# Gate and up products of two FFN half-steps as Strassen blocks, with the down product in three partial passes

## The chip, the cores and the metric

The kernel runs on one core of one Trainium2 chip. The metric is the device time of one execution in microseconds (us); a kernel is judged by the median of its runs. Five engines work side by side and meet at semaphores: PE (TensorE, the matrix products; its weight loads are listed apart as PEld), DVE (VectorE), ACT (ScalarE), POOL (GpSimd) and SP (SyncE), which here only issues DMAs. Each engine works through its own instructions in a fixed order.

## The reference

One layer of a sequence model on x of 512 tokens by 1024 features, in float32:

```python
def swiglu(h, w_gate, w_up, w_down):
    return (jax.nn.silu(h @ w_gate) * (h @ w_up)) @ w_down

x = x + 0.5 * swiglu(rms_norm(x, ffn1_norm), ffn1_w_gate, ffn1_w_up, ffn1_w_down)
x = x + hybrid_mixer(x, ...)
x = x + 0.5 * swiglu(rms_norm(x, ffn2_norm), ffn2_w_gate, ffn2_w_up, ffn2_w_down)
return rms_norm(x, final_norm)
```

`w_gate` and `w_up` are 1024 x 2816, `w_down` is 2816 x 1024. The mixer projects the normed x to 3600 columns, runs a state-space scan on 16 heads and banded attention on 8, and projects back with `w_out`. The change leaves the mixer's arithmetic as it is.

## The kernel before

Activations lie feature-major: 128 features on the partitions, 512 tokens along them, so the model width is 8 tiles (KD) and the FFN width 22 tiles (NF). Every float32 operand of a product is split into two float32r parts, hi and lo, and every product is three matmuls, hi·hi, hi·lo and lo·hi (`mm3`, L130 to L133).

Weights come through `Stream` (L101 to L126): `prepare` has SP load a piece into one of three `raw` buffers, and `wsplit` (L94 to L99) makes the parts, the hi part by a cast on ACT (L96), the lo part by a subtraction on DVE (L98), 128x512 at a time. `get` keeps three pieces ahead of the one in use.

`ffn` (L217 to L256) is one SwiGLU half-step. For each of 22 feature tiles it runs the gate product (`proj` into a PSUM tile of tag `mm`) and the up product (into `aux`): 8 contraction tiles x 3 matmuls of 512 columns each, 48 for both. DVE then multiplies each by the norm's factor (L234, L238), ACT takes the silu (L236), DVE multiplies the two (L240), and ACT and DVE split the result into parts (L242, L243). The norm is not applied to x ahead of the product: `split_act` (L136 to L139) scales x by the norm's weight as it splits it, and the factor 1/sqrt(mean) of a token comes from `rstd_begin` and `rstd_end` (sums of squares on ACT and DVE, L143 to L147, then small DVE steps L154 to L162, diagonals L187, and two matmuls L194 that spread them). Behind all 22 tiles the down product runs 8 output features, each 22 contraction tiles x 3 matmuls in one PSUM accumulation, and one DVE instruction adds it to x (L255).

The first tile of FFN 1 stands apart (L289 to L305), interleaved with the arrival of x. Ahead of FFN 2 the second part of the output projection (L808 to L822) adds to x (L820) and splits x for FFN 2. In the last feature of FFN 2 (`last2`) the halves of the tokens go one after the other, by 132 matmuls of 256 columns, so that the final norm of one half lies beside the product of the other.

The order on each engine is that of the program, moved by a scheduler that knows the data and buffers. POOL makes constants at the start, the decay products of the scan (L432) and the bias tiles of attention (L706); in the two FFNs it has nothing.

Of the kernel before, what the change touches and what calls it, by code (L numbers as in the profile page):

```python
# [8 lines left out]
F32 = mybir.dt.float32  # L9
# [21 lines left out]
# columns of the packed per-partition parameter array  # L31
# [6 lines left out]
def hybrid_block(ctx: ExitStack, tc, xT, par, wgu1, wd1, win, wdt, wv, wo, rbt, wgu2, wd2, out):  # L38
# [30 lines left out]
    # the tensor engine's clock rises after some time of work: constants, until the first data is there  # L69
# [6 lines left out]
    # triLE[s, l] = 1 where s <= l ; gt[s', s] = 1 where s' > s  # L76
# [5 lines left out]
    gtf = sb("fa", [P, P], bufs=2)  # L82
# [3 lines left out]
    # onl[:, 0]: first 64 columns one, onl[:, 1]: last 64 columns one  # L86
# [14 lines left out]
    class Stream:  # L101
        """Weights in the order in which they are used: loaded in pieces of up to 4 KB a partition,
        split exactly into two float32r parts in halves of those, some halves ahead of their use."""

        def __init__(self, look=3):
            self.src, self.done, self.used, self.look, self.raw = [], [], 0, look, None

        def add(self, dram, n, c):
            """dram: [128, n, c]"""
            sub = SEQ // c  # L110
            for a in range(0, n, sub):
                self.src.append((dram if a == 0 else None, n, c, a, min(n, a + sub)))

        def prepare(self):
            dram, n, c, a, b = self.src[len(self.done)]
            if dram is not None:
                self.raw = sb("raw", [P, n, c], bufs=3)
                nc.sync.dma_start(out=self.raw, in_=dram)
            self.done.append(wsplit(self.raw[:, a:b]))
# [29 lines left out]
    def rsqrt_tiny(v, n):  # L149
        """v^-1/2 on [128, n]"""  # L150
# [20 lines left out]
    def rstd_begin(acc, n):  # L171
        """1/sqrt(mean + eps) per token: on the diagonals of [128, tile, 128], and as columns"""
# [6 lines left out]
    def diag_parts(r, n, dh, dl):  # L179
        """columns r as diagonals, in two exact parts"""  # L180
# [22 lines left out]

    def xw_tiles():
        return ([sb(f"xwh{k}", [P, SEQ], F32R) for k in range(KD)],
                [sb(f"xwl{k}", [P, SEQ], F32R) for k in range(KD)])

# [1 line left out]
    def ffn_weights(wgu, wd, f0=0, o1=KD):  # L209
        for ft in range(f0, NF):  # L210
            ws.add(wgu[ft, 0], KD, P)
            ws.add(wgu[ft, 1], KD, P)
        for o in range(o1):
            for a, b in ((0, 8), (8, 16), (16, 22)):
                ws.add(wd[o, :, a:b, :], b - a, P)

    def ffn(xh, xl, norm, hslots, after, first=None, last=None):  # L217
        hh, hl = [], []
        for ft in range(NF):
            if ft == 0:  # L220
                pss = first or [proj(xh, xl, mmps()), proj(xh, xl, aux())]
                # the norm's factor comes between the next tile's products
                dg = None if first else norm()
                nxt = [proj(xh, xl, mmps())]
                dg = dg or norm()
                if first:
                    nxt.append(proj(xh, xl, aux()))
                rs = rstd_end(dg)
            elif ft == 1:
                pss = nxt if first else nxt + [proj(xh, xl, aux())]  # L230
            else:
                pss = [proj(xh, xl, mmps()), proj(xh, xl, aux())]
            a = sb("fa", [P, SEQ], bufs=2)
            V.tensor_tensor(out=a, in0=pss[0], in1=rs, op=ALU.mult)  # L234
            s = sb("fs", [P, SEQ], bufs=2)
            S.activation(out=s, in_=a, func=AF.Silu)  # L236
            u = sb("fu", [P, SEQ], bufs=2)
            V.tensor_tensor(out=u, in0=pss[1], in1=rs, op=ALU.mult)  # L238
            h = sb("fh", [P, SEQ], bufs=2)
            V.tensor_tensor(out=h, in0=s, in1=u, op=ALU.mult)  # L240
            hi, lo = hslots[ft]()
            S.copy(out=hi, in_=h)  # L242
            V.tensor_tensor(out=lo, in0=h, in1=f(hi), op=ALU.subtract)  # L243
            hh.append(hi)
            hl.append(lo)
        for o in range(KD):
            if o == KD - 1 and last:
                last(hh, hl)
                break
            ps = mmps()  # L250
            for a in range(0, NF, 4):
                wh, wl = ws.get()
                for k in range(a, min(a + 4, NF)):
                    mm3(ps, wh[:, k - a], wl[:, k - a], hh[k], hl[k], k == 0, k == NF - 1)
            V.scalar_tensor_tensor(out=x[:, o], in0=ps, scalar=0.5, in1=x[:, o], op0=ALU.mult, op1=ALU.add)  # L255
            after(o)  # L256

    def proj(xh, xl, ps):
        for k in range(KD):
            if k % 4 == 0:  # L260
                wh, wl = ws.get()
            mm3(ps, wh[:, k % 4], wl[:, k % 4], xh[k], xl[k], k == 0, k == KD - 1)
        return ps

    # slots that are also used side by side as one tile
# [66 lines left out]
    ffn(x1h, x1l, norm1, [pair_slot(2 * i, 2 * i + 1) for i in range(NF)], after1, first=first)  # L332
    xh, xl = x2
# [1 line left out]
    # order of the feature tiles of the projection (win is laid out in the same order)  # L335
# [17 lines left out]
    def proj_gen(ah, al, done):  # L353
        """one feature tile, in pieces of two contraction tiles"""
# [11 lines left out]
    def conv(ci, dst, ps):  # L366
        u = sb("fa", [P, SEQ], bufs=2)
# [15 lines left out]
    def bc(g):  # L383
        """B and C of a group, of which the first is evacuated after most of the second's products"""
# [8 lines left out]
    def bc_products(g):  # L393
        # token-major B of the first three chunks
# [6 lines left out]
        # C.B products with s <= l: cbm[g][s, c, l]  # L401
# [34 lines left out]
    def ssd_in(st):  # L436
# [3 lines left out]
        # token-major x * dt  # L440
# [7 lines left out]
        # D skip, in place of the feature-major x  # L448
# [504 lines left out]
```

## Time and profile before

| | us |
|---|---|
| median of 3 runs (lowest, highest) | 1075.79 (1075.69, 1076.99) |
| span of the profiled execution | 1074.0 |
| FFN 1, first tile | 0 to 18 |
| FFN 1, rest | 18 to 368 |
| projections, scan, attention | 368 to 681 |
| second part of the output projection | 681 to 700 |
| FFN 2 and final norm | 700 to 1074 |

The runs lie some 1.8 us above the span of the profiled execution, which counts from its first instruction to its last. How to read the tables: "busy" is the time in which an engine had an instruction in work; the matmuls overlap in their pipeline, so that one lasts 0.39 us and yet a new one starts each 0.23 us, and the step from start to start is the rate. The clock column is the TensorE clock that was granted, 1.00 for the upper of its two levels, 2.4 GHz.

### The profile page before, as it was taken

To read this page: it belongs to the slowest core of one execution; us is meant where nothing else is said; L and a number is where in the kernel's file an instruction comes from. 1 tells how busy PE (TensorE), PEld (TensorE's weight loads), DVE (VectorE), ACT (ScalarE), POOL (GpSimd) and SP (SyncE) were. 2 spreads that over 40 slices of the span, in tenths; PEclk is the share of its full clock that TensorE was granted. 3 is DMA by queue.
4 is the path that set the end of the run, shared out by engine and by line. 5 is a ranking of instruction groups with operands and counts; after the bars stand their busy time and mean duration, and the time that the engine had idled before them with its cause. 6 is when DMAs were issued, how large, how long until landed. Compare 5 with 4: busy or idle time off the path is not lost.

```text
span 1074.0 us, 13004 instructions
## 1 busy us (share of the span) xinstructions
PE 1059.9 (99%) x4922; PEld 868.4 (81%) x4922; DVE 609.5 (57%) x1131; ACT 463.9 (43%) x805; POOL 56.5 (5%) x61
## 2 busy tenths in 40 slices
PE   9999999999999999999999999999999999999996
PEld 7888888888888787878887777888888888888886
DVE  6644445453334398978858888864444445433333
ACT  6433333333323356646747855543333333333331
POOL 0000000000000003332110111000000000000000
PEclk9999999999999999999999999999999999999998
DMA  6223333223233221212221222223322222333322
GB/s 223 96 98 98 98 99 99 98 93 93 89 98 99 98 79 59 79 60 79 80 98 61 77 81 81 92 81 99 99 98 98 98 99 98 94 89 101 100 69 79
DMA packets 31518, 99.54 MB, mean 93 GB/s; under 512 B 3296, under 2 KB 5600, under 8 KB 31456
## 3 DMA queue, kind: packets, MB, share of 16 engines
q1 hardware_dynamic: 29216, 95.69, 28.0%
q10 hardware_dynamic: 2240, 3.02, 0.9%
q8 instruction: 38, 0.62, 0.2%
q14 instruction: 24, 0.20, 0.1%
HBM read 96.61 MB, written 2.10 MB: 92 GB/s over the span
## 4 chain that ended last, share of the span: by engine, by line
PE 92%; DVE 6%; ACT 1%; issue 0%; DMA 0%; DVEq 0%; ACTq 0%
PE mm L131 21%; PE mm L132 21%; PE mm L133 20%; PE aux L131 8%; PE aux L132 8%; PE aux L133 8%; DVE fs L377 2%; PE aux L759 1%; PE aux L737 1%; DVE wlo L98 1%; PE aux L719 1%; PE aux L501 0%; PE aux L718 0%; PE aux L461 0%; DVE fa L368 0%
## 5 line engine op out<-in xcount | busy, mean ns | idle before, releaser
L96 ACT CAST whi<-raw 128x512 fp32r<-128x512 f32 x354 | 216.3, 612 | 426.1 <-PE mm L132 256.3
L98 DVE TENSOR_TENSOR wlo<-raw,whi 128x512 fp32r<-128x512 f32 x354 | 244.6, 692 | 219.4 <-ACT whi L96 217.9
L131 PE MATMUL mm<-xwh,whi 128*128 128x512 f32 x520 | 209.1, 402 | 1.5 <-ACT whi L96 1.5
L132 PE MATMUL mm<-xwl,whi 128*128 128x512 f32 x520 | 203.5, 391 | 0.0
L133 PE MATMUL mm<-xwh,wlo 128*128 128x512 f32 x520 | 203.0, 390 | 0.0
L131 PE MATMUL mm<-s,whi 128*128 128x512 f32 x482 | 187.7, 390 | 0.0
L132 PE MATMUL mm<-s,whi 128*128 128x512 f32 x482 | 187.7, 389 | 0.0
L133 PE MATMUL mm<-s,wlo 128*128 128x512 f32 x482 | 187.6, 389 | 0.0
L131 PEld LDWEIGHTS mm<-xwh,whi 128*128 128x128 f32 x520 | 98.0, 188 | 23.7 <-issue 2.8
L133 PEld LDWEIGHTS mm<-xwh,wlo 128*128 128x128 f32 x520 | 97.6, 188 | 20.8
L132 PEld LDWEIGHTS mm<-xwl,whi 128*128 128x128 f32 x520 | 97.8, 188 | 20.2 <-issue 1.2
L133 PEld LDWEIGHTS mm<-s,wlo 128*128 128x128 f32 x482 | 90.5, 188 | 19.1
L131 PEld LDWEIGHTS mm<-s,whi 128*128 128x128 f32 x482 | 90.5, 188 | 19.0 <-ACT s L763 0.2
L132 PEld LDWEIGHTS mm<-s,whi 128*128 128x128 f32 x482 | 90.4, 188 | 18.8 <-DVE s L764 0.2
L131 PE MATMUL aux<-xwh,whi 128*128 128x512 f32 x176 | 68.7, 390 | 0.0
L133 PE MATMUL aux<-xwh,wlo 128*128 128x512 f32 x176 | 68.6, 390 | 0.0
L132 PE MATMUL aux<-xwl,whi 128*128 128x512 f32 x176 | 68.5, 389 | 0.0
L131 PE MATMUL aux<-s,whi 128*128 128x512 f32 x176 | 68.5, 389 | 0.0
L133 PE MATMUL aux<-s,wlo 128*128 128x512 f32 x176 | 68.5, 389 | 0.0
L132 PE MATMUL aux<-s,whi 128*128 128x512 f32 x176 | 68.5, 389 | 0.0
L238 DVE TENSOR_TENSOR fu<-aux,rstd 128x512 f32<-128x512 f32 x44 | 30.4, 691 | 62.5 <-PE aux L133 62.5
L234 DVE TENSOR_TENSOR fa<-mm,rstd 128x512 f32<-128x512 f32 x44 | 30.4, 691 | 60.5 <-PE mm L133 60.5
(234 smaller groups left out, 1203.1 us busy)
## 6 DMA issues: line engine op xcount, KB each, us to landing
raw<-wgu SPq DMA_DIRECT2D x86, 512.0 KB, 3.3
raw<-wd SPq DMA_DIRECT2D x32, 512.0 KB, 3.5
raw<-win SPq DMA_DIRECT2D x28, 512.0 KB, 3.3
raw<-wd SPq DMA_DIRECT2D x16, 384.0 KB, 3.1
raw<-wo SPq DMA_DIRECT2D x12, 512.0 KB, 3.6
x<-xT SPq DMA_DIRECT2D x8, 256.0 KB, 5.1
raw<-wv SPq DMA_DIRECT2D x4, 512.0 KB, 3.9
fu<-rbt ACTq DMA_DIRECT2D x8, 256.0 KB, 2.7
```

Source lines behind the costliest of these rows:

```text
L96: S.copy(out=hi, in_=src)
L98: V.tensor_tensor(out=lo, in0=src, in1=f(hi), op=ALU.subtract)
L131: T.matmul(ps, lhsT=sh, rhs=mh, start=start, stop=False)
L132: T.matmul(ps, lhsT=sh, rhs=ml, start=False, stop=False)
L133: T.matmul(ps, lhsT=sl, rhs=mh, start=False, stop=stop)
L234: V.tensor_tensor(out=a, in0=pss[0], in1=rs, op=ALU.mult)
L238: V.tensor_tensor(out=u, in0=pss[1], in1=rs, op=ALU.mult)
L377: V.scalar_tensor_tensor(out=y[:, d:SEQ], in0=u[:, 0:SEQ - d], scalar=cw(j), in1=y[:, d:SEQ], op0=ALU.mult, op1=ALU.add)
L719: T.matmul(psx[:, 0:w], lhsT=q2[rows, isl], rhs=kl[rows, 0:w], start=False, stop=True)
L737: T.transpose(out=pp[:, kt * P:(kt + 1) * P], in_=pr[:, kt * P:(kt + 1) * P], identity=ident)
L759: T.matmul(po[:, kt * P:SEQ], lhsT=v2, rhs=p[:, kt, kt * P:SEQ], start=(n == 0), stop=(n == len(todo) - 1))
```

## The change

The gate and up products of a tile become one 2x2 block product. The weights of a tile are blocks by output (gate, up) and by contraction half (k tiles 0 to 3 and 4 to 7); x is blocked by contraction half and by token half (256 columns). Eight block products become seven, P1 to P7 (a Winograd form of Strassen's), each of 4 contraction tiles x 3 matmuls of 256 columns, 84 of 256 columns for 48 of 512. This asks for sums of blocks:

- Of weights, four 128x512 sums a tile on POOL (`S21`, `S43` of `GateUp`), each pair of sums split as a 128x1024 piece by `wsplit8` (ACT cast L262, DVE subtraction L264). The gate weights are split so too (`G`); only half of the up weights is split as it is (`U`, by the old `wsplit`, now L101 and L103).
- Of x, once for each FFN (`XCombos`): DVE scales x by the norm's weight (L353), POOL makes the sums (L366, L369, L372), ACT and DVE split them (L349, L350).
- Of products: PSUM holds two running sums, ACT copies three of them out (L420), DVE combines them (L422, L424, L426, L432, L433); the silu's result is multiplied by the norm's factor on POOL (L429).

```diff
+    def wsplit8(src):
...
+        hi = sb(f"xw{2 * i}", [P, KD, P], F32R)
+        S.copy(out=hi, in_=src)
+        lo = sb(f"xw{2 * i + 1}", [P, KD, P], F32R)
+        V.tensor_tensor(out=lo, in0=src, in1=f(hi), op=ALU.subtract)
...
+        def G(self):
+            self.g = load(self.wgu[self.ft, 0], KD, P)
+            return wsplit8(self.g)
+        def S21(self):
+            self.u = load(self.wgu[self.ft, 1], KD, P)
...
+            G.tensor_tensor(out=self.s[:, 4:8], in0=self.u[:, 0:4], in1=self.u[:, 4:8], op=ALU.add)
+            G.tensor_tensor(out=self.s[:, 0:4], in0=self.s[:, 4:8], in1=self.g[:, 0:4], op=ALU.subtract)
+            return wsplit8(self.s)
+        def S43(self):
+            G.tensor_tensor(out=self.s[:, 0:4], in0=self.g[:, 4:8], in1=self.s[:, 0:4], op=ALU.subtract)
+            G.tensor_tensor(out=self.s[:, 4:8], in0=self.g[:, 0:4], in1=self.u[:, 0:4], op=ALU.subtract)
+            return wsplit8(self.s)
+        def U(self):
+            return wsplit(self.u[:, 4:8])
...
+    def schedule(f0, f1, first):
...
+                out += [("P1", ft), ("P7", ft - 1), ("P2", ft), ("P6", ft), ("P5", ft), ("P3", ft - 1), ("P4", ft - 1)]
...
+        def run(p, ft):
...
+            for k in range(4):
+                mh, ml = xc.moving(p, k)
+                for n, (sw, m) in enumerate(((wh, mh), (wh, ml), (wl, mh))):
+                    T.matmul(ps, lhsT=sw[:, a + k], rhs=m, start=(p in ("P1", "P2", "P5") and k == 0 and n == 0),
+                             stop=(k == 3 and n == 2), skip_group_check=True)
+            if p in ("P1", "P6", "P7"):
+                S.copy(out=abc[:, ("P1", "P6", "P7").index(p)], in_=X)
+            if p == "P7":
+                V.tensor_tensor(out=abc[:, 0::2], in0=W.rearrange("p (a b) -> p a b", a=2), in1=abc[:, 0::2], op=ALU.add)
+            elif p == "P3":
+                V.tensor_tensor(out=abc[:, 1], in0=W[:, HI], in1=abc[:, 1], op=ALU.add)
...
+                V.tensor_tensor(out=g, in0=g, in1=rs[0], op=ALU.mult)
...
+                S.activation(out=s, in_=g, func=AF.Silu)
+                G.tensor_tensor(out=s, in0=s, in1=rs[0], op=ALU.mult)
+            elif p == "P4":
...
+                V.tensor_tensor(out=h[:, LO], in0=X, in1=d["s"][:, LO], op=ALU.mult)
+                V.tensor_tensor(out=h[:, HI], in0=d["s"][:, HI], in1=abc[:, 2], op=ALU.mult)
+                finish(ft, h)
```

`finish` splits h as before (now L401, L402). The first tile of FFN 1 stays at eight products, its first four contraction tiles by halves of the tokens. The sums of x need room, so the 22 tiles go in blocks of 8, 8 and 6 (`BLOCKS`), each with its own partial down pass over its tiles for all 8 features, which adds to x on DVE three times for once. `raw` has four buffers for three. At the end of FFN 2 three features instead of one go by halves of the tokens, of the last block alone: 108 matmuls of 256 columns for 132, and two more additions and squares.

DVE on one tile, before (`wlo` and `whi` are weight parts, `raw` the loaded weights, `mm` and `aux` PSUM tiles, `rstd` the norm's factor):

```order
L98 TENSOR_TENSOR wlo_656<-raw_652,whi_654 128x512
L234 TENSOR_TENSOR fa_705<-mm_635,rstd_363 128x512
L98 TENSOR_TENSOR wlo_673<-raw_652,whi_671 128x512
L98 TENSOR_TENSOR wlo_691<-raw_687,whi_689 128x512
L238 TENSOR_TENSOR fu_709<-aux_670,rstd_363 128x512
L98 TENSOR_TENSOR wlo_720<-raw_687,whi_718 128x512
L240 TENSOR_TENSOR fh_711<-fs_707,fu_709 128x512
L243 TENSOR_TENSOR s_171_714<-fh_711,s_170_713 128x512
```

and a tile of the second block after the change (`xw` are the 128x1024 weight parts, `s_72` the sums that POOL made; the three L264 rows are S43 of the tile before, then G and S21 of a coming tile, and L103 is U):

```order
L422 TENSOR_TENSOR fa_1782<-aux_1781,fa_1782 128x2x256
L402 TENSOR_TENSOR s_313_1904<-fh_1900,s_312_1903 128x512
L264 TENSOR_TENSOR xw_323_1963<-s_72_325,xw_322_1961 128x1024
L103 TENSOR_TENSOR wlo_2293<-raw_2134,whi_2291 128x512
L264 TENSOR_TENSOR xw_338_2058<-raw_2054,xw_337_2056 128x1024
L424 TENSOR_TENSOR fa_1782<-aux_1781,fa_1782 128x256
L264 TENSOR_TENSOR xw_327_2013<-s_72_325,xw_326_2011 128x1024
L426 TENSOR_TENSOR fa_1782<-fa_1782,rstd_482 128x512
L432 TENSOR_TENSOR fh_2027<-mm_1780,fs_2004 128x256
L433 TENSOR_TENSOR fh_2027<-fs_2004,fa_1782 128x256
```

The four 128x512 subtractions of a tile became three of 128x1024 and one of 128x512, two of them from what POOL wrote, and the four other instructions became six, three of 256 columns.

POOL on the same tile after the change, where it had no instruction before:

```order
L281 TENSOR_TENSOR s_72_325<-raw_2134 128x512
L282 TENSOR_TENSOR s_72_325<-s_72_325,raw_2054 128x512
L287 TENSOR_TENSOR s_72_325<-raw_1927,s_72_325 128x512
L288 TENSOR_TENSOR s_72_325<-raw_1927,raw_2007 128x512
L429 TENSOR_TENSOR fs_2004<-fs_2004,rstd_482 128x512
```

The first two make S21 of a coming tile, the next two S43 of the tile at hand, and L429 stands behind them all.

DVE where FFN 2 is prepared, before: four instructions for each feature of the output projection (`x` is the residual, `acc` the sum of squares):

```order
L820 TENSOR_TENSOR x_62<-x_62,mm_6048 128x512
L98 TENSOR_TENSOR wlo_6071<-raw_6067,whi_6069 128x512
L139 SCALAR_TENSOR_TENSOR s_1394_5986<-x_62,par_61,s_1393_5985 128x512
L147 TENSOR_TENSOR acc_5997<-acc_5997,fh_6064 128x512
```

and after, in the second half of the features (`fu` and `s_1419` hold sums that POOL made of x):

```order
L1036 TENSOR_TENSOR x_62<-x_62,mm_7215 128x512
L350 TENSOR_TENSOR s_1406_7056<-s_1418_7068,s_1405_7055 128x256
L350 TENSOR_TENSOR s_25_109<-s_1419_7069,s_25_109 128x512
L153 TENSOR_TENSOR acc_7073<-acc_7073,fh_7205 128x512
L350 TENSOR_TENSOR s_1412_7062<-fu_7208,s_1411_7061 128x512
L353 TENSOR_SCALAR s_1420_7070<-x_62,par_61 128x512
L350 TENSOR_TENSOR s_1408_7058<-s_1419_7069,s_1407_7057 128x256
```

One split of x became a scaling and four splits, of which all but one wait for a sum from POOL.

## Rows read from the trace of the kernel before

**Rows 1.** The page: busy time of each engine; engines of the chain that ended last.

```profile
PE 1059.9 (99%) x4922; PEld 868.4 (81%) x4922; DVE 609.5 (57%) x1131; ACT 463.9 (43%) x805; POOL 56.5 (5%) x61
...
PE 92%; DVE 6%; ACT 1%; issue 0%; DMA 0%; DVEq 0%; ACTq 0%
```

**Rows 2.** Windows, FFN 1 and 2: us, busy PE, PEld, DVE, ACT, POOL, PE clock, DMA share, GB/s.

```profile
28.90:256.60 227.70, 227.70 (x1006) 188.52 (x1005) 110.78 (x173) 80.88 (x130) 0.00 (x0) 1.00 0.30 96
699.80:939.00 239.20, 239.20 (x1061) 198.13 (x1060) 117.69 (x193) 85.50 (x137) 0.00 (x0) 1.00 0.30 96
```

**Rows 3.** PE's timeline in FFN 1 (start us, us, engine, line, tiles); 11 alike left out.

```profile
99.79 0.39 PE L131 MATMUL mm<-xwh,whi 128*128 128x512 f32 x1
...
102.51 0.39 PE L131 MATMUL aux<-xwh,whi 128*128 128x512 f32 x1
```

**Rows 4.** PE's timeline in the last feature, halves of the tokens; 43 alike left out.

```profile
1049.65 0.28 PE L131 MATMUL mm<-xwh,s 128*128 128x256 f32 x1
...
1054.93 0.28 PE L133 MATMUL mm<-s,s 128*128 128x256 f32 x1
```

**Rows 5.** DVE's timeline in FFN 1, POOL idle.

```profile
25.79 0.16 DVE L160 SCALAR_TENSOR_TENSOR rq_r<-rq_q,rq_v 128x4 f32<-128x4 f32 x1
25.99 0.16 DVE L162 SCALAR_TENSOR_TENSOR rq_o<-rq_r,rq_y 128x4 f32<-128x4 f32 x1
...
31.22 0.69 DVE L234 TENSOR_TENSOR fa<-mm,rstd 128x512 f32<-128x512 f32 x1
31.82 0.68 DVE L238 TENSOR_TENSOR fu<-aux,rstd 128x512 f32<-128x512 f32 x1
```

**Rows 6.** Instruction groups by form, DVE and ACT: count, busy us, mean ns, idle before.

```profile
L98 DVE TENSOR_TENSOR wlo<-raw,whi 128x512 fp32r<-128x512 f32 x339 | 238.2, 704 | 193.9 <-ACT whi L96 192.4 <-PE aux L194 1.0
L508 DVE TENSOR_TENSOR s<-s,s 128x128 f32<-128x128 f32 x24 | 9.7, 441 | 0.0
L506 DVE TENSOR_TENSOR s<-s,aux 128x128 f32<-128x128 f32 x32 | 7.8, 278 | 0.5 <-PE aux L501 0.5
L466 DVE COPY dt<-s 128x4 f32<-128x4 f32 x12 | 7.0, 581 | 4.9 <-ACT s L463 4.8
L98 DVE TENSOR_TENSOR wlo<-raw,whi 128x256 fp32r<-128x256 f32 x15 | 6.4, 425 | 25.5 <-ACT whi L96 25.5
L729 DVE TENSOR_SCALAR s<-s,ri 128x512 f32<-128x512 f32 x8 | 3.9, 482 | 0.1
L96 ACT CAST whi<-raw 128x512 fp32r<-128x512 f32 x339 | 210.2, 621 | 396.6 <-PE mm L132 226.8 <-PE aux L132 137.1 <-PE aux L133 12.9
```

**Rows 7.** POOL's timeline in the scan.

```profile
415.46 1.04 POOL L432 TENSOR_TENSOR fu<-dt,tri 128x512 fp32r<-128x512 f32 x1 [9.86 <-PE aux L461]
...
428.99 1.48 POOL L432 TENSOR_TENSOR fh<-dt,tri 128x512 fp32r<-128x512 f32 x1
430.43 1.48 POOL L432 TENSOR_TENSOR fu<-dt,tri 128x512 fp32r<-128x512 f32 x1
```

**Rows 8.** DVE's timeline beside the last two of these.

```profile
429.49 0.28 DVE L506 TENSOR_TENSOR s<-s,aux 128x128 f32<-128x128 f32 x1
429.69 1.32 DVE L98 TENSOR_TENSOR wlo<-raw,whi 128x512 fp32r<-128x512 f32 x1
```

**Rows 9.** Instruction groups by form, POOL: count, busy us, mean ns, idle before.

```profile
L432 POOL TENSOR_TENSOR fh<-dt,tri 128x512 fp32r<-128x512 f32 x16 | 21.8, 1366 | 18.2 <-DVE acc L147 18.2
L432 POOL TENSOR_TENSOR fu<-dt,tri 128x512 fp32r<-128x512 f32 x16 | 19.4, 1220 | 464.4 <-DVE dt L655 397.6 <-PE aux L483 44.7 <-PE aux L461 22.1
L706 POOL TENSOR_SCALAR fh<-fu 128x512 f32<-128x512 f32 x8 | 12.7, 1589 | 120.7 <-DMA fu<-rbt 41.9 <-DVE wlo L98 31.8 <-DVE acc L147 31.1
```

**Rows 10.** Timelines: first work on x (ACT), first tile's end (PE), first addition of L820 (DVE).

```profile
4.88 0.72 ACT L138 ACTIVATE xwh<-x,par 128x512 fp32r<-128x512 f32 x1 [2.05 <-DMA par<-par]
...
17.87 0.39 PE L133 MATMUL aux<-xwh,wlo 128*128 128x512 f32 x1
...
681.65 0.69 DVE L820 TENSOR_TENSOR x<-x,mm 128x512 f32<-128x512 f32 x1 [0.81 <-PE mm L133]
```

More of the change, by code (lines that the diff above doesn't have):

```diff
@@ L105, in __init__, with piece @@
         def __init__(self, look=3):
-            self.src, self.done, self.used, self.look, self.raw = [], [], 0, look, None
+            self.jobs, self.done, self.used, self.look = [], [], 0, look
         def add(self, dram, n, c):
             sub = SEQ // c
[L111 to L119, printed above, removed]
+            raw = []
+            def piece(a, b):
+                if not raw:
+                    raw.append(load(dram, n, c))
+                return wsplit(raw[0][:, a:b])
+            jobs = [lambda a=a, b=min(n, a + sub): piece(a, b) for a in range(0, n, sub)]
+            self.jobs += jobs
+            return jobs
         def get(self):
@@ L202, in rstd_end, with xw_pair @@
         return rs
+    def xw_pair(k):
+        t = sb(f"xw{k}", [P, 2, SEQ], F32R)
+        return t[:, 0], t[:, 1]
     def xw_tiles():
[L205 to L263, printed above, removed]
+        p = [xw_pair(k) for k in range(KD)]
+        return [hi for hi, _ in p], [lo for _, lo in p]
     wide = {}
@@ new lines, in schedule @@
+    def schedule(f0, f1, first):
+        out = []
+        for ft in range(f0, f1):
+            if first and ft == f0:
+                out += [("P1", ft), ("P1", ft + 1), ("P2", ft), ("P2", ft + 1), ("P6", ft), ("P5", ft)]
+            elif first and ft == f0 + 1:
+                out += [("P7", ft - 1), ("P6", ft), ("P5", ft), ("P3", ft - 1), ("P4", ft - 1)]
+            else:
+                out += [("P1", ft), ("P7", ft - 1), ("P2", ft), ("P6", ft), ("P5", ft), ("P3", ft - 1), ("P4", ft - 1)]
+        return out
@@ new lines, in hybrid_block, with ffn_weights, gate_up @@
+    PIECE = {"P1": ("G", 0), "P2": ("G", 4), "P6": ("S21", 0), "P5": ("S21", 4), "P7": ("S43", 4), "P3": ("S43", 0),
+             "P4": ("U", 0)}
+    def ffn_weights(wgu, wd, f0, last=0):
+        made, seen = {}, set()
+        def gate_up(sched):
+            for p, ft in sched:
+                kind = PIECE[p][0]
+                if (kind, ft) not in seen:
+                    seen.add((kind, ft))
+                    job = made.setdefault(ft, GateUp(wgu, ft))
+                    ws.jobs.append(getattr(job, kind))
+        for n, (a, b) in enumerate(BLOCKS):
+            gate_up(schedule(max(a, f0) if n == 0 else a + 1, min(b + 1, NF), n == 0))
+            if n == 2:
+                gate_up([("P7", NF - 1), ("P3", NF - 1), ("P4", NF - 1)])
+            at = len(ws.jobs)
+            for o in range(KD - last if n == 2 else KD):
+                ws.add(wd[o, :, a:b, :], b - a, P)
+            if n == 2:
+                u, j = ws.jobs[at - 1], ws.jobs[at:]
+                ws.jobs[at - 1:] = [j[0], u, j[2], j[1], j[3]] + j[4:]
@@ L299, in hybrid_block @@
     for k in range(KD):
-        split_act(x[:, k], pt[:, C_F1 + k:C_F1 + k + 1], x1h[k], x1l[k])
+        xc1.weigh(x[:, k], k)
+        xc1.base(k)
+        if k < 4:
+            xc1.split(xc1.half(b12, k), xc1.xw[k][:, HI])
         if k % 4 == 0:
             pieces = [wsplit(raws[j][:, k:k + 4]) for j in range(2)]
+        xc1.sums(k)
         for j in range(2):
             wh, wl = pieces[j]
-            mm3(first[j], wh[:, k % 4], wl[:, k % 4], x1h[k], x1l[k], k == 0, k == KD - 1)
+            if k < 4:
+                for h, t in ((LO, xc1.b1), (HI, b12)):
+                    mh, ml = xc1.half(t, k)
+                    for n, (sw, m) in enumerate(((wh, mh), (wh, ml), (wl, mh))):
+                        T.matmul(first[j][:, h], lhsT=sw[:, k], rhs=m, start=(k == 0 and n == 0 and h is LO), stop=False,
+                                 skip_group_check=True)
+            else:
+                mm3(first[j], wh[:, k % 4], wl[:, k % 4], *xc1.b2[k - 4], False, k == KD - 1, skip=True)
+        if k >= 4:
+            xc1.parts(k - 4)
+            xc1.parts(k)
     S.dma_start(out=dtw, in_=wdt)
@@ L331, in hybrid_block @@
     ffn_weights(wgu1, wd1, 1)
-    ffn(x1h, x1l, norm1, [pair_slot(2 * i, 2 * i + 1) for i in range(NF)], after1, first=first)
+    ffn(xc1, norm1, 1, after1, first=first)
     xh, xl = x2
@@ L820, in hybrid_block @@
         V.tensor_tensor(out=x[:, o], in0=x[:, o], in1=ps, op=ALU.add)
[L821 removed]
+        xc3.weigh(x[:, o], o)
+        xc3.base(o)
         add_squares(accs[1], x[:, o], o == 0)
[L825 to L826 removed]
+        xc3.sums(o)
+        xc3.parts(o)
+    NL = 3
     def after2(o):
@@ L867, in last2 @@
             pv = aux()
-            for t in range(2):
-                tt = slice(half * H + t * P, half * H + (t + 1) * P)
-                T.matmul(pv[:, t:t + 1], lhsT=sq[:, tt], rhs=ones[:, 0:1], start=True, stop=True)
+            for i, src in enumerate((accs[2], sq)):
+                for t in range(2):
+                    tt = slice(half * H + t * P, half * H + (t + 1) * P)
+                    T.matmul(pv[:, 2 * i + t:2 * i + t + 1], lhsT=src[:, tt], rhs=ones[:, 0:1], start=True, stop=True)
```

234 lines of the change are left out of this document (182 added, 52 removed).

## The prediction

> **What bounds the kernel now.** I read the page first, then the windows of the FFNs, then single instructions. PE is busy 99% of the span and makes 92% of the chain that ended last [rows 1]. In the gate and up stages of both FFNs PE is busy in every microsecond, 227.70 of 227.70 and 239.20 of 239.20, at a granted clock of 1.00, the upper level, while DVE is busy in half of that time, ACT in a third and POOL never [rows 2]. Here time goes only with PE's work, or comes if something makes PE wait. The profiled execution has a span of 1074.0 us; the median lies 1.8 us above it.
>
> **What PE saves.** A matmul of 512 columns starts each (102.51 − 99.79) / 12 = 0.2267 us [rows 3], one of 256 each (1054.93 − 1049.65) / 44 = 0.1200 us [rows 4]: more than half, so seven eighths of the columns do not cost seven eighths of the time. A tile goes from 48 × 0.2267 = 10.88 us to 84 × 0.1200 = 10.08: −0.80. With 21 tiles in FFN 1 (its first keeps eight products) and 22 in FFN 2, −34.4 us. In that first tile 24 matmuls of 512 become 48 of 256: +0.3. The last features do 108 matmuls of 256 columns for 132 while the rest of the down product stays the same in sum; what more stands at the end (two additions and squares a half) I put at +0.2. Together +0.5.
>
> **What DVE does now.** Alone, its 512-column instruction takes 0.69 us and the next starts 0.60 later; tiny ones follow at 0.20 [rows 5]. The 256-column subtraction has a mean 0.28 below the 512-column one [rows 6], so I take 0.34 for 256 columns and 0.60 + 2 × 0.267 = 1.13 for 1024. Scaling by a column (a tensor_scalar) has a mean of 0.48 [rows 6]; less the same overlap 0.39. A tile now asks of DVE 3 × 1.13 + 3 × 0.60 + 0.34 with both inputs in SBUF and 0.60 + 2 × 0.34 with one in PSUM, 6.8 us in PE's 10.08. Alone it fits.
>
> **What POOL does to DVE.** POOL gets five 512-column instructions a tile. Alone one takes 1.04 us; where they run in a row beside DVE's work, one starts each 1.44 us and lasts 1.48 [rows 7]. Beside these DVE's subtraction from SBUF takes 1.32 us for 0.69, while one that reads PSUM keeps its 0.28 [rows 8]. So a POOL instruction and a DVE instruction on SBUF take 1.45 together, 0.85 above DVE's own 0.60. That is the upper price of a POOL instruction in a chain that DVE fills. The lower one is from the means, of instructions that met by chance. On DVE: the subtraction 339 × (0.704 − 0.69) = 4.7 us, the copy of four columns 12 × (0.581 − 0.16) = 5.1, the 128-column product 24 × (0.441 − 0.278) = 3.9 [rows 5, 6], 13.7 us over POOL's 40 large instructions, 0.34 each; on POOL the decay products' means, 1.366 and 1.220, lie 0.25 above 1.04 [rows 9]. In a chain through both engines that is 0.59, call it 0.6. If DVE's gaps take POOL's work it is nothing.
>
> The Trainium skill (SBUF — State Buffer, "Who interferes with whom") has a rule for this: DVE instructions with two SBUF inputs and GpSimd instructions that read SBUF hold a shared port pair in turn, each for its whole length, and an operand in PSUM frees DVE of it. The trace agrees on who meets whom, by the subtraction and the PSUM instruction just named; not on the length, since 1.45 us for a pair is less than 1.04 + 0.60. With 1.0 us each everywhere the sums below would give some 1112 us.
>
> **The starts.** Here DVE is full, so I take 0.85. In FFN 1, work on x begins at 4.9 us [rows 10]. Until the norm's factor is ready DVE has, by its order, 8 scalings, 16 subtractions of 256 columns, 24 instructions of 512, 6 of 1024 and 15 tiny ones: 3.1 + 5.4 + 14.4 + 6.8 + 3.0 = 32.7, so it ends at 37.6. PE needs the factor behind the first tile, whose last matmul starts at 17.9 [rows 10] and is done by 18.1, the 0.3 above, and 104 products: 18.4 + 12.5 = 30.9. Loss 6.7 without POOL. POOL's sums of x come to 8 full instructions and its sums of weights to 8 in that stretch: 16 × 0.85 = 13.6. Loss **20.3**.
>
> In FFN 2, from the first addition of the output projection at 681.7 [rows 10], DVE has 33 of 512 columns, 8 scalings, 13 of 256, 7 of 1024 and 14 tiny: 38.0 us. PE has 18.1 us to the end of that projection at 699.8 and 137 products, 16.4: 34.6. Loss 3.4 without POOL. POOL has 8 for x and 12 for weights; some six fall among the first features, where DVE still waits for PE. 14 × 0.85 = 11.9. Loss **15.3**.
>
> **Steady tiles.** DVE and POOL wait for one another in a ring: the split of S43, U, G, the addition of P3, the split of S21 (1.13 + 0.60 + 1.13 + 0.34 + 1.13 = 4.33), then POOL's two sums for S43 and its product behind the silu (3.0), then DVE's two products, the PSUM addition and the split of h (2.0): 9.35 us a tile, under PE's 10.08. ACT's casts (0.62 for 512 columns [rows 6]) lie beside it. Two further POOL instructions, the sums for the next S21, fall among DVE's splits. DVE has gaps here, so I take 0.6: 10.55, or 0.47 above PE. A block that follows a down pass starts with splits made ahead: the first S43 part is there 1.13 + 2.0 + 1.24 + 1.13 + 0.6 = 6.1 us into the tile and wanted after eight products, 11.5: 5.4 us of lead, which covers 8 × 0.47. The first block of each FFN, behind a late start, has none: 13 tiles × 0.47 = **6.1**.
>
> Nothing for the down passes: the sum of their matmuls is the same, each of DVE's 16 further additions per FFN takes 0.6 beside 5.4 us of PE's (24 × 0.2267), and three `mm` buffers keep PE from waiting for it. Loads: the same weights, once each, at a DMA share of 0.30 [rows 2].
>
> Sum: 1074.0 − 34.4 + 0.5 + 20.3 + 15.3 + 6.1 = 1081.8, and 1.8 to the median: **1083.6 us**. The two starts eat what PE saves.
>
> **Rivals.**
> - *PE stays the bound (the other side).* POOL's sums fall into DVE's gaps and cost DVE nothing: 1074.0 − 34.4 + 0.5 + 6.7 + 3.4 + 1.8 = **1052.0**. For it: DVE is busy half the time now and has 3.3 us of each tile to spare. Against it: the scan's rows, and that DVE is full in both starts. The side changes where losses reach 33.9 us. With one price c for each POOL instruction they are 10.1 + 30c + 13 × (2c − 0.73): at c = 0.6, 34.2. So 0.6 us decides.
> - *Mild everywhere.* 0.6 in the starts too: 6.7 + 9.6 and 3.4 + 8.4, with 6.1 in the tiles 34.2: **1076.1**, no change.
> - *Full price everywhere.* At 0.85 the ring takes 11.05, 0.97 above PE: 12.6 in the first blocks and 2 × (8 × 0.97 − 5.4) = 4.7 in the second. Losses 20.3 + 15.3 + 17.3: **1094.8**. The Trainium skill's exclusive pair, cited above, lies on this side.
> - *POOL slower on streams of weights.* A POOL instruction from SBUF with a mean of 1.59 exists [rows 9]. At 0.5 more on three of them in the ring, 12.05: 1.97 a tile, 25.6 + 2 × (15.8 − 5.4) + 2 × (11.8 − 5.4) = 59.2 with the starts' 35.6: **1136.7**.
>
> **How the numbers follow.** The forecast, starts contended and tiles mildly so, 0.32, with its own range 1076 to 1092 (starts' price 0.6 to 1.0). PE stays the bound 0.26, and it reaches to 1065 as c goes to 0.4. Mild everywhere 0.18, 1068 to 1080. Full price 0.13. Slower POOL 0.08. The rest, 0.03, is anything else, a clock that falls in a start included. A measurement here tells 0.2%, 2.2 us, from no change. Faster: the 0.26, 0.12 of the mild case and 0.05 of the forecast's lower edge, 0.43. Same: 0.08. Slower: 0.49. The range goes from 1048 to 1106: it leaves out the slower POOL, the rest, the lowest quarter of PE's case and the highest of the full price.
>
> **What the profile would show.** Right: PE waits for DVE's `xw` and `s` parts in the first 52 us and between 682 and 735; DVE's 1024-column splits last well over 1.2 us, and POOL's sums 1.4 to 1.5; the spread matmuls start near 50 us for 29.9 now; later tiles stand at 10.1 to 10.6 us. Wrong: PE full from 20 us on (then 1052), tiles at 11 us or more in the middle of a block (then 1095 or beyond), a granted clock under 1.00 in the starts, or 256-column matmuls off 0.120 us.

## The result and the profile after

The changed kernel takes 1189.35 us (median of 4 runs, 1186.52 to 1190.9), the kernel before 1076.38 in the same series: a ratio of 1.1045, 95% interval 1.1027 to 1.1062. The forecast was 1083.6 us, with a range to 1106. The sign was that of the likeliest case, the size was missed by 106 us, and even the dearest rival (1136.7) lies 53 us short.

The page of the changed kernel, with the lines that answer to [rows 1], and the clock by slices:

```profile
PE 1072.0 (90%) x6482; PEld 944.4 (80%) x6482; DVE 846.2 (71%) x1295; ACT 552.5 (47%) x963; POOL 414.2 (35%) x300
...
PEclk8898999999999999999999999879999999999998
...
PE 40%; DVE 22%; POOL 13%; issue 10%; DMA 10%; ACT 5%; SPq 1%; DVEq 0%; POOLq 0%; ACTq 0%
DMA raw<-wgu 9%; PE mm L137 9%; PE mm L138 9%; PE mm L139 9%; DVE xw L264 6%; POOL s L287 4%; POOL s L288 3%; PE mm L417 3%; DVE wlo L103 3%; PE aux L417 3%; DVE s L350 2%; DVE fs L597 2%; POOL s L281 2%; POOL s L282 2%; ACT whi L101 1%
```

PE has lost the chain: from 92% to 40%, the rest in DVE, POOL and, a thing that stood at 0% before, the loads of the gate and up weights, 9%. The windows of FFN 1 (us, busy PE, PEld, DVE, ACT, POOL, clock, DMA share, GB/s), as in [rows 2]:

```profile
20.00:60.00 40.00, 26.36 (x141) 22.68 (x142) 37.92 (x48) 16.75 (x28) 22.02 (x16) 0.78 0.14 48
60.00:139.00 79.00, 67.09 (x506) 65.17 (x505) 59.11 (x64) 35.61 (x57) 45.59 (x28) 0.94 0.23 79
139.00:187.00 48.00, 48.00 (x231) 40.49 (x231) 24.62 (x33) 13.75 (x21) 9.86 (x7) 1.00 0.34 103
187.00:281.00 94.00, 80.88 (x632) 78.65 (x632) 63.84 (x73) 40.46 (x67) 51.31 (x34) 0.96 0.25 82
```

The start, the tiles of the first block, its down pass, the tiles of the second. In the down pass PE is full; in the tiles it stands idle for 12 to 13 us in each window, and in the start a third of the time, at a granted clock of 0.78. The step from one tile's silu to the next is the time of a tile; at the beginning of the second block:

```profile
198.72 0.63 ACT L428 ACTIVATE fs<-fa 128x512 f32<-128x512 f32 x1 [2.76 <-DVE fa L426]
212.27 0.63 ACT L428 ACTIVATE fs<-fa 128x512 f32<-128x512 f32 x1 [3.43 <-DVE fa L426]
226.01 0.63 ACT L428 ACTIVATE fs<-fa 128x512 f32<-128x512 f32 x1 [2.40 <-DVE fa L426]
```

A tile takes 12.42 to 16.42 us in the first block of FFN 1 and 13.5 to 13.7 at the beginning of the later ones, for 10.55 and 10.08 forecast; in the blocks of 8 only the last two run at 9.6, with tiles of 12.4 to 12.9 before them. The mixer between the FFNs is as long as before: its decay products on POOL stand 58.9 us later from first to last.

The span of the profiled execution grew by 110.7 us, to 1184.7; with the 33.9 that PE saves, 144.6 were lost. The spread matmuls of the norm's factor start at 57.2 us in FFN 1 (26.3 behind PE's own 30.9) and at 798.5 in FFN 2 (22.9 behind the first addition at 741.0 plus 34.6):

```profile
57.17 0.77 PE L200 MATMUL aux<-s,onesr 128*128 128x512 f32 x1 [2.79 <-DVE s L193]
741.01 0.69 DVE L1036 TENSOR_TENSOR x<-x,mm 128x512 f32<-128x512 f32 x1 [0.82 <-PE mm L139]
798.48 0.40 PE L200 MATMUL aux<-s,onesr 128*128 128x512 f32 x1
```

So the starts hold 49 us, and by difference the tiles hold some 95.

The chain through one tile of the second block, in order of time (start, us, what):

```profile
211.71 1.68 POOL s L287
213.39 1.26 POOL s L288
214.65 0.02 issue
214.67 0.33 SPq L96
215.00 0.04 issue
215.04 4.66 DMA raw<-wgu
219.70 0.02 issue
219.72 0.63 ACT whi L101
220.35 0.02 issue
220.37 0.06 DVE wlo L103
220.44 1.16 issue
221.60 2.32 DVE xw L264
223.91 0.33 DVE fa L424
224.25 1.14 DVE xw L264
225.39 0.07 issue
225.46 1.68 POOL s L287
```

The name after each time is the engine (SPq is SP's queue issuing the load), then tile and line. From L287 to L287 it is 13.75 us. PE does not appear. POOL makes S43, which is the last reader of a tile's raw weights; then SP may load into that buffer, which takes 4.66 us; then come ACT's cast, DVE's splits of U, G and S21; then POOL's next S43. Two more views show why the splits are long. DVE in that stretch:

```profile
220.37 1.30 DVE L103 TENSOR_TENSOR wlo<-raw,whi 128x512 fp32r<-128x512 f32 x1 [0.87 <-ACT whi L101]
221.60 2.32 DVE L264 TENSOR_TENSOR xw<-raw,xw 128x1024 fp32r<-128x1024 f32 x1
223.84 0.41 DVE L424 TENSOR_TENSOR fa<-aux,fa 128x256 f32<-128x256 f32 x1
224.17 1.21 DVE L264 TENSOR_TENSOR xw<-s,xw 128x1024 fp32r<-128x1024 f32 x1
225.30 0.68 DVE L426 TENSOR_TENSOR fa<-fa,rstd 128x512 f32<-128x512 f32 x1
```

and POOL:

```profile
219.83 1.29 POOL L281 TENSOR_TENSOR s<-raw 128x512 f32<-128x512 f32 x1 [3.97 <-DMA raw<-wgu]
221.20 1.63 POOL L282 TENSOR_TENSOR s<-s,raw 128x512 f32<-128x512 f32 x1
225.46 1.68 POOL L287 TENSOR_TENSOR s<-raw,s 128x512 f32<-128x512 f32 x1 [2.62 <-DVE xw L264]
227.09 1.29 POOL L288 TENSOR_TENSOR s<-raw,raw 128x512 f32<-128x512 f32 x1
```

Two things are to be seen. L288 takes 1.29 us while DVE does nothing at all (its next instruction starts at 229.65): that, and not 1.04 [rows 7], is POOL's price alone for such a sum. And the two engines take turns by whole instructions. DVE's L103 (0.68 alone) ends 0.55 behind the end of L281; L282 can work only then and ends at 222.83; DVE's 1024-column split, 1.21 alone, ends 1.09 behind that, and so lasts 2.32. The Trainium skill (SBUF — State Buffer, "Who interferes with whom") has it so, each for its whole length; this trace agrees but for a small rest. L103 and L282 together take 1.71 us (221.12 to 222.83), 0.18 under 0.60 + 1.29, as the forecast's 1.45 for a pair lay 0.19 under 1.04 + 0.60. That gap was no reason to set the rule aside.

### The profile page after: what moved, and what is told of

Same layout as the page of the kernel before. It is cut to its first block, busy times and chain, and to the rows that moved or that the text cites. A ratio compares the mean times of both kernels' runs of the same rounds, so it can differ in the third digit from the quotient of the medians.

```text
span 1184.7 us, 16774 instructions
## 1 busy us (share of the span) xinstructions
PE 1072.0 (90%) x6482; PEld 944.4 (80%) x6482; DVE 846.2 (71%) x1295; ACT 552.5 (47%) x963; POOL 414.2 (35%) x300
## 4 chain that ended last, share of the span: by engine, by line
PE 40%; DVE 22%; POOL 13%; issue 10%; DMA 10%; ACT 5%; SPq 1%; DVEq 0%; POOLq 0%; ACTq 0%
DMA raw<-wgu 9%; PE mm L137 9%; PE mm L138 9%; PE mm L139 9%; DVE xw L264 6%; POOL s L287 4%; POOL s L288 3%; PE mm L417 3%; DVE wlo L103 3%; PE aux L417 3%; DVE s L350 2%; DVE fs L597 2%; POOL s L281 2%; POOL s L282 2%; ACT whi L101 1%
## 5 line engine op out<-in xcount | busy, mean ns | idle before, releaser
L417 PE MATMUL aux<-s,xw 128*128 128x256 f32 x1548 | 224.5, 299 | 54.5 <-DVE fa L422 54.5
L417 PEld LDWEIGHTS aux<-s,xw 128*128 128x128 f32 x1548 | 209.1, 205 | 61.9 <-DVE fa L422 61.4
L103 DVE TENSOR_TENSOR wlo<-raw,whi 128x512 fp32r<-128x512 f32 (+1 forms) x225 | 193.9, 865 | 74.2 <-ACT whi L101 73.5
L417 PE MATMUL mm<-s,xw 128*128 128x256 f32 x1548 | 208.6, 288 | 31.5 <-ACT fa L420 13.8
L417 PEld LDWEIGHTS mm<-s,xw 128*128 128x128 f32 x1548 | 196.8, 195 | 37.4 <-ACT fa L420 15.8
L101 ACT CAST whi<-raw 128x512 fp32r<-128x512 f32 (+1 forms) x225 | 135.2, 605 | 183.8 <-PE mm L138 125.6
L281 POOL TENSOR_TENSOR s<-raw 128x512 f32<-128x512 f32 x43 | 67.8, 1577 | 251.2 <-DMA raw<-wgu 180.6
L264 DVE TENSOR_TENSOR xw<-s,xw 128x1024 fp32r<-128x1024 f32 x86 | 114.1, 1326 | 28.2 <-ACT xw L262 27.0
L137 PE MATMUL mm<-xw,whi 128*128 128x512 f32 x288 | 118.7, 413 | 0.0
L138 PE MATMUL mm<-xw,whi 128*128 128x512 f32 x288 | 113.1, 393 | 0.0
L139 PE MATMUL mm<-xw,wlo 128*128 128x512 f32 x288 | 112.8, 392 | 0.0
L262 ACT CAST xw<-s 128x1024 fp32r<-128x1024 f32 x86 | 90.1, 1047 | 48.3 <-POOL s L288 18.1
L287 POOL TENSOR_TENSOR s<-raw,s 128x512 f32<-128x512 f32 x43 | 72.2, 1679 | 66.3 <-DVE xw L264 62.0
L429 POOL TENSOR_TENSOR fs<-fs,rstd 128x512 f32<-128x512 f32 x43 | 58.4, 1357 | 89.1 <-ACT fs L428 89.1
L401 ACT CAST s<-fh 128x512 fp32r<-128x512 f32 x44 | 27.2, 619 | 121.3 <-DVE fh L433 120.0
L432 DVE TENSOR_TENSOR fh<-mm,fs 128x256 f32<-128x256 f32 x43 | 18.1, 420 | 91.1 <-POOL fs L429 91.1
```

Of the source, the lines that this page charges most:

```text
L101: S.copy(out=hi, in_=src)
L103: V.tensor_tensor(out=lo, in0=src, in1=f(hi), op=ALU.subtract)
L137: T.matmul(ps, lhsT=sh, rhs=mh, start=start, stop=False, skip_group_check=skip)
L138: T.matmul(ps, lhsT=sh, rhs=ml, start=False, stop=False, skip_group_check=skip)
L139: T.matmul(ps, lhsT=sl, rhs=mh, start=False, stop=stop, skip_group_check=skip)
L262: S.copy(out=hi, in_=src)
```

## The experiments

Times are device us; the kernel before stood beside them at 1075.5 to 1076.8. Runs without an interval are single.

**No weight sums.** POOL's four sums are taken out of `S21` and `S43`:

```diff
...
-            G.tensor_tensor(out=self.s[:, 4:8], in0=self.u[:, 0:4], in1=self.u[:, 4:8], op=ALU.add)
...
-            return wsplit8(self.s)
+            return wsplit8(self.u)
...
-            return wsplit8(self.s)
+            return wsplit8(self.g)
```

> POOL's four weight sums of a tile are left out; the splits that took S21 and S43 take the loaded up and gate weights instead, so the products are of other numbers, with the same matmuls, splits and loads. Theory (the ring through POOL): the changed kernel's tiles stand 13.5 us apart because DVE's splits wait for POOL's sums, POOL's sums for DVE's splits, and both stretch each other; without the sums the tiles fall to PE's 10.1 us and only the starts lose, some 15 and 11 us, beside POOL's sums of x: 1060 to 1080 us. Rival (DVE's own order, with loads into four buffers): DVE issues as much as before and loads come no earlier, tiles stay above 12.5 us, over 1150.

1072.6 us. Tiles inside a block from silu to silu at 10.08, the spread matmuls of FFN 1 at 47.8, and PE busy in all of the second block (the columns of the windows above):

```profile
187.00:260.00 73.00, 73.00 (x515) 68.83 (x514) 43.93 (x64) 32.47 (x54) 7.93 (x6) 1.00 0.32 102
```

The tiles lose nothing without the sums, the saving of 0.80 a tile on PE is real, and what is left is in the starts (16.9 us in FFN 1, 11.6 in FFN 2), which are 21 us less than in the changed kernel.

**Sums made, but read by nobody.** The four sums stay, and the splits take the raw weights as above.

> POOL makes all its sums, but nothing reads them: the splits take the loaded weights instead, as in the run without sums. This parts the two prices of the sums. If the ring (waiting for results) is most of it, this kernel comes near the one without sums, under 1100 us. If it is that POOL's and DVE's instructions hold each other up when they meet, it stays near the changed kernel, over 1150. Theory: both, DVE's 6.8 us of a tile plus five meetings of 1.0 to 1.1 give 12 us a tile, some 1130.

1211.0 us, slower than the change and outside what the theory gave. That nothing waits for a sum saves nothing. POOL in two tiles:

```profile
218.37 1.27 POOL L429 TENSOR_TENSOR fs<-fs,rstd 128x512 f32<-128x512 f32 x1
226.73 1.29 POOL L281 TENSOR_TENSOR s<-raw 128x512 f32<-128x512 f32 x1 [7.09 <-DMA raw<-wgu]
228.10 1.62 POOL L282 TENSOR_TENSOR s<-s,raw 128x512 f32<-128x512 f32 x1
...
232.31 1.27 POOL L429 TENSOR_TENSOR fs<-fs,rstd 128x512 f32<-128x512 f32 x1
```

The period is 13.94: POOL's five instructions, 6.9, and 7.1 of waiting for a load. The sums still read the raw buffers and hold them, and with POOL's product in line behind them DVE waits too (5.05 us for L429 in the second of these tiles). So the loads look like a ring of their own with POOL, which pointed to the buffers.

**Sums on DVE.** `G.tensor_tensor` becomes `V.tensor_tensor` in the four lines.

> The four weight sums of a tile go from POOL to DVE; POOL keeps the sums of x and the product behind the silu. Theory: DVE has 6.8 + 4 x 0.60 = 9.2 us a tile without meetings, under PE's 10.1, so tiles fall to 10.1 to 10.8 us and the starts lose some 20 each: 1075 to 1105 us, 80 us or more better than the change. Rival (the length of DVE's queue is what PE waits for): 2.4 us more on DVE make tiles longer, above 1189.

1101.7 us, 88 less than the change, with some 2.4 us more work on DVE in each tile (4 × 0.60). Tiles inside the later blocks at 10.4 to 10.7. The rival, DVE's length, falls.

**The silu's product on DVE.** L429 alone, from G to V.

> Only the product behind the silu goes from POOL to DVE, where it costs 0.60. In the changed kernel it stands on POOL behind two sums, and DVE's queue stands 3.7 us waiting for it. Theory: the ring becomes shorter by about 2.5 us in the tiles that stood at 13.5, some 30 of them: 1110 to 1130 us. Rival (the sums' own length and the meetings set the pace, the silu's place does not): within 15 us of the change's 1189.

1194.0 us: the theory's 1110 to 1130 missed, the rival held. Tiles stand at 14.0 to 14.2, and POOL's group for the first sum tells why (count, busy us, mean ns, idle before and who ended it):

```profile
L281 POOL TENSOR_TENSOR s<-raw 128x512 f32<-128x512 f32 x43 | 67.2, 1564 | 309.4 <-DMA raw<-wgu 288.4 <-DVE xw L264 20.1 <-DVE rq_q L164 0.9
```

The wait for loads grew from 180.6 us to 288.4. The reading: the product was in one ring, the loads in another of nearly the same length, and opening one leaves the other. The next two runs test it.

**Six raw buffers**, to open the loads' ring:

```diff
-        raw = sb("raw", [P, n, c], bufs=4)
+        raw = sb("raw", [P, n, c], bufs=6)
...
-        rs = sb("rstd", [P, SEQ], bufs=2)
+        rs = sb("rstd", [P, SEQ], bufs=1)
...
```

> Six raw buffers for four (the norm's factor gets one buffer for two, to make room). In the changed kernel's chain a tile of 13.5 us goes: load 4.4, cast 0.6, DVE's splits 5.1, POOL's two S43 sums 3.0, 0.3 to issue, next load; the buffers come free only when S43 has been made. Theory: with two more buffers the load leaves that chain, the ring through POOL and DVE without it is 11.5 to 12.5 us, and some 24 tiles gain 1 to 2 us each: 1135 to 1165 us. Rival (loads wait, but what sets the pace is the meeting of POOL and DVE alone): within 10 us of 1189.

1167.9 us, 21 less, 3 us outside the expected; tiles at 12.9. About half of the gain lies in the starts, whose spread matmuls now come 23.6 and 15.0 us late, for 26.3 and 22.9. DMA in the chain of waits falls from 10% to 1%:

```profile
PE 49%; DVE 20%; POOL 17%; issue 9%; ACT 4%; DMA 1%; POOLq 0%; DVEq 0%; ACTq 0%
```

**Six buffers and the product on DVE.**

> Six raw buffers and the product behind the silu on DVE together. Alone the second gave nothing (1194), and its tiles of 14.0 us stood on the load's ring. Theory of two rings of about one length: with both opened, what is left is DVE's own row of instructions with their meetings, 10.8 to 11.3 us a tile: 1105 to 1135 us, clearly under the six buffers alone. Rival: the product's place is worth nothing there either, the time equals that of six buffers alone within 10 us.

1148.3 us, another 20 less, where the product alone had given nothing. The two rings are shown by the four runs together (1189, 1194, 1168, 1148). The size was missed: tiles at 12.2, not 11. In such a tile four DVE instructions meet a sum of POOL's: L264 lasts 1.99 us for 1.22 alone, L426, L103 and L429 1.75 to 1.78 for 0.69, 4.0 us in all.

**Meetings alone.** The kernel without sums, with four POOL instructions behind the silu's product that nobody waits for and that read no raw weights (and write what nobody reads):

```diff
+                z = wide_tile(40, F32)
+                for n in range(4):
+                    G.tensor_tensor(out=z[:, n], in0=s, in1=rs[0], op=ALU.subtract)
```

> The kernel without weight sums, and four more POOL instructions behind the silu's product of each tile, of the same size, reading its result and the norm's factor and writing to a tile that nothing reads: POOL has its five instructions a tile again, but no split waits for them and no load's buffer is held by them. What is left is the meetings alone. Theory (shared access for two SBUF operands, one at a time): 5.5 us of DVE and 6.5 of POOL exclude each other, 12 us a tile where there is no lead: 1110 to 1140 us against 1073 without the four. Rival (meetings alone are absorbed; it is the held buffers and waits): 1073 to 1085.

1158.0 us, 85 more than without the four. Most tiles at 11.96 to 11.99, the 12 that were expected. The time lies above the range: the tiles at the ends of blocks, too, take 10.8 to 11.1. The starts come as in the run without sums (spread matmuls 17.0 and 11.7 us late), so the difference lies in the tiles. DVE's groups and POOL's:

```profile
L264 DVE TENSOR_TENSOR xw<-raw,xw 128x1024 fp32r<-128x1024 f32 x129 | 211.0, 1650 | 19.0 <-ACT xw L262 18.9
```

```profile
L426 POOL TENSOR_TENSOR s<-fs,rstd 128x512 f32<-128x512 f32 x172 | 275.5, 1632 | 3.4
L423 POOL TENSOR_TENSOR fs<-fs,rstd 128x512 f32<-128x512 f32 x43 | 56.2, 1308 | 377.2 <-ACT fs L422 377.2
```

The split's mean goes from 1226 ns (without the four) to 1650, POOL's from 1308 for L423, in which DVE mostly waits for it, to 1632. This is the larger part: 85 of the change's 117 us over the run without sums. Of the other 31, some 21 lie in the starts and by difference some 10 in the tiles. These are not the price of the rings alone, since opening both gave 41.

**The same four in the scan's form.** Their operands repeat four columns and 128 columns over 512, as the decay products do:

```diff
-                    G.tensor_tensor(out=z[:, n], in0=s, in1=rs[0], op=ALU.subtract)
+                    G.tensor_tensor(out=z[:, n].rearrange("p (a b) -> p a b", a=4), in0=s[:, 0:4].unsqueeze(2).broadcast_to([P, 4, P]),
+                                    in1=rs[0][:, 0:P].unsqueeze(1).broadcast_to([P, 4, P]), op=ALU.mult)
```

> As the run with four more POOL instructions a tile (1157.96), but the four take their operands in the form of the scan's decay products, four columns and 128 columns each repeated over 512, for two full streams of 512; nothing reads their results. The forecast priced POOL's instructions by the scan's row, 1.04 us alone; in the changed kernel they take 1.26 to 1.30 with DVE idle. Theory: the form of the operands makes the difference, 4 x 0.25 = 1.0 us a tile less: tiles at 11.0 for 12.0, some 35 us less than 1158. Rival: they take 1.3 here too, since it is something else in these stages, and the time stays within 10 us of 1158.

1116.6 us, 41 less; most tiles at 10.96 to 11.02, as expected.

```profile
L426 POOL TENSOR_TENSOR s<-fs,rstd 128x512 f32<-128x512 f32 x172 | 232.1, 1379 | 3.4
```

A mean of 1379 for 1632 beside the same DVE work. The operands' form is worth 0.25 us (the operation, a product for a subtraction, is not it: a product of two full operands, L429 in the changed kernel, takes 1.26 as well), and the row that the forecast took was of the cheap form. The trace's names and sizes don't show it: both rows read 128x512 from two operands.

**All on DVE.** Weight sums, sums of x and L429, POOL idle in both FFNs.

> POOL has nothing in the FFNs: weight sums, sums of x and the product behind the silu are all on DVE. No meetings, and DVE has 6.8 + 2.4 + 0.6 = 9.8 us in a tile of 10.1. Theory (the starts of the run with the weight sums on DVE, 1101.7, still lost by meetings with the sums of x and the silu's product): 1070 to 1090 us. Rival (DVE too full: the starts and the first block lose as much as the meetings did): 1100 us or more.

1077.0 us, beside 1076.8 of the kernel before: no difference that single runs can show. Tiles of the later blocks at 10.0 to 10.3. But the spread matmuls of FFN 1 start at 53.0 and the first block's tiles take 10.8 to 11.3: the spread matmuls come 22.1 and 11.8 us late, 33.9 together: what PE saves, the two starts take back, without a sum on POOL.

**First block by eight products.** So the sums of x were moved out of the start. In a version with all sums on DVE, the first block of each FFN keeps eight products, and the sums of x are made during its tiles 1 to 4:

```diff
+            if 1 <= ft < 5:
+                for k in (ft - 1, ft + 3):
+                    xc.sums(k)
+                for k in (ft - 1, ft + 3):
+                    xc.parts(k)
...
+            if n == 0:
+                for ft in range(f0, b):
+                    ws.add(wgu[ft, 0], KD, P)
+                    ws.add(wgu[ft, 1], KD, P)
```

> A version made from what the runs showed. POOL has nothing in the FFNs (all sums on DVE), and the first block of 8 tiles of each FFN keeps eight products, with x's parts by token halves for the first four contraction tiles; the sums of x are made on DVE during tiles 1 to 4, where a plain tile leaves DVE some 6 us free. The second and third blocks (14 tiles of each FFN) go by seven products. Theory (the run with everything on DVE, 1076.95, lost in its two starts and first blocks what 43 tiles saved, while its later blocks ran at 10.1 us): 28 x 0.80 = 22 us saved, 15 plain tiles cost 0.3 each: 1057 to 1068 us. Rival (the second block's beginning, now without lead, loses as much as the first did): 1072 us or more.

1061.4 us, ratio 0.986 (0.9844 to 0.9877): inside the expected.

**Blocks of 6, 8 and 8.**

```diff
-    BLOCKS = ((0, 8), (8, 16), (16, 22))
+    BLOCKS = ((0, 6), (6, 14), (14, 22))
```

> The same with blocks of 6, 8 and 8 tiles, so 16 tiles of each FFN go by seven products, and the last block that goes by token halves has 8 tiles. Theory: 4 more tiles save 0.80 + 0.3 each, 4 us less than the version with 8, 8 and 6, less about 1 us for the longer part by halves. Rival (a shorter first block leaves the sums of x late): no better than that version.

1056.7 us, ratio 0.9817 (0.9803 to 0.9832). It beats both kernels. Its page, and the windows of the start, of the stretch with the first down pass, and of the first tiles by seven products:

```profile
PE 1040.5 (99%) x6368; PEld 919.8 (87%) x6368; DVE 809.2 (77%) x1461; ACT 537.0 (51%) x934; POOL 57.1 (5%) x61
...
0.00:60.00 60.00, 57.21 (x350) 52.14 (x351) 48.72 (x105) 35.47 (x70) 2.01 (x13) 0.97 0.47 156
60.00:120.00 60.00, 60.00 (x337) 52.72 (x336) 35.67 (x54) 21.69 (x35) 0.00 (x0) 1.00 0.31 92
120.00:180.00 60.00, 60.00 (x502) 60.00 (x501) 56.01 (x84) 33.10 (x53) 0.00 (x0) 1.00 0.31 106
```

PE is full again in the down pass and in the tiles by seven products, beside a DVE that is busy for 93% of the last window.

**That version with the weight sums back on POOL**, four raw buffers.

> The version with blocks of 6, 8 and 8 (1056.73, first block by eight products, all sums on DVE), with the four weight sums of a tile back on POOL, four raw buffers: the starts are out of it. Theory: each of the 32 tiles by seven products goes back to 12.5 to 13.5 us, less what a lead covers at the beginning and end of a block, so about 2 us each on average: 1105 to 1140 us. If it stays under 1075, the changed kernel's loss was one of its starts.

1151.1 us: 94 us for the place of four sums in 32 tiles, more than expected; tiles at the beginning of a block at 13.9 to 14.5. The starts are out of it (the spread matmuls of FFN 1 at 34.5, for 35.0 with the sums on DVE), so the change's loss is in its tiles first.

## Why the prediction was wrong

- **PE's saving was right.** 10.08 us a tile, to the hundredth, where nothing keeps PE (the run without sums). So was what DVE needs alone: 1.13 for 1024 columns, 1.14 in the chain above.
- **"Alone one takes 1.04 us" was mis-sized.** The row was of operands that repeat a few columns; a sum of two full operands takes 1.26 to 1.30. On four sums and a product that is 1.2 us a tile; the run in the scan's form gave 41 us for four of the five. The Trainium skill (GPSIMD Engine Reference, "3.1 Elementwise — side-by-side cycle accounting") gives some 2.6 cycles an element for two inputs at 1.2 GHz, an estimate of 1.1 us for 512; the rows here lie above it, and the scan's row below.
- **"DVE has gaps here, so I take 0.6" was wrong, and it is the largest term.** POOL and DVE shut each other out by nearly whole instructions, 5.5 us of DVE and 6.5 of POOL in a tile, and the sum, 12.0, is what the tiles of the run with meetings alone took, above PE's 10.08. The price itself was not far off: the four instructions raised DVE's busy time from 750.3 to 877.7 us, 0.74 for each of 172. But the forecast charged it for two of the five in a tile, put the other three into its ring at 1.0 as if nothing met them, and so had the tile only 0.47 above PE. The gaps are small: without the four, DVE waits 1.3 us in a tile for ACT's casts. In a tile with them its instructions last 3.3 us longer, and 1.9 of it reach the tile. That made 85 us for a forecast of 6.1 in tiles; 41 of the 85 hang on the mis-sized instruction above.
- **"Loads: the same weights, once each, at a DMA share of 0.30" failed as a reason for nothing.** The share says what the queue could carry, not when it may. The last reader of a raw buffer used to be a split that runs pieces ahead; now it is POOL's S43, behind S21's split. Load and its wait, some 5 us, came into a ring that I had drawn without them. Opening it was worth 21 us alone, half of it in the starts, and 41 with the product's ring opened too.
- **The lead of 5.4 us did not carry a block**, since a tile lost 3.4 us and not 0.47: two tiles use it up. In the second block PE is busy 23.86 of 25.27 us between 187 and 212.27, and 11.01 of 13.74 up to 226.01.
- **The starts were right in kind and small in size**: 26.3 and 22.9 for 20.3 and 15.3. DVE's tiny steps of the norm met POOL as well: L158, 128x4, took 1.26 us for 0.16, beside L282:

```profile
48.18 1.63 POOL L282 TENSOR_TENSOR s<-s,raw 128x512 f32<-128x512 f32 x1
48.58 1.26 DVE L158 TENSOR_SCALAR rq_t<-rq_v 128x4 int32<-128x4 int32 x1
```

The held buffers have a part in it too: with six of them the starts lose 23.6 and 15.0. What the longer POOL instruction (1.3 for 1.04) adds there was not separated. That the starts, even without a meeting, eat what PE saves was shown by the run with all on DVE, 1077.0, with 22.1 and 11.8; the forecast had 6.7 and 3.4 for that, which left out that the sums would then be DVE's.
- **The rivals.** "PE stays the bound" needs a price under 0.6 a POOL instruction; it was 0.74 on DVE. "Slower POOL", with 0.08 of chance, had the error's direction, a longer POOL instruction, but neither the load in the ring nor the number of meetings, and no other rival had these either.

## What to carry to other kernels

Before work is given to an idle POOL, add its time and the time of DVE's instructions with both operands in SBUF over the period of the stage: if the sum is above what the bounding engine needs, POOL is not idle capacity, and the same work on DVE itself can be faster (here 1101.7 for 1189.4). The sum is a lower bound: with six buffers and the product on DVE it is 11.3 us and the tiles took 12.2. For each buffer of a load ask who reads it last after the change; a low DMA share is no reason to leave a load out of a ring. And an operation that saves PE time only after a preparation can begin one block late: the preparation then lies under other work, which here turned 1077 into 1057.

## What the runs showed of the hardware

A POOL sum of two 128x512 operands from SBUF takes 1.26 to 1.30 us alone; with operands that repeat columns 1.04 [rows 7]. A DVE instruction on SBUF that meets it waits for its end even when it is tiny (1.26 us for 4 columns), and POOL's waits for DVE's in turn (1.63 to 1.68 for 1.29). Between 20 and 60 us the granted clock was 0.78, a mean over stretches at 1.2 and at 2.4 GHz, while PE was busy for 26.36 of 40 us; what that cost was not separated from the waits.
